# Batched matmul, 32 x (512 x 1024) x (1024 x 768): most output stores cover four batches instead of two

## The chip, the cores and the metric

The kernel runs on one core of a Trainium2 chip. A core has a matrix engine (PE), a vector engine (DVE), a scalar engine (ACT), a general engine (POOL) and a queue engine (SP), and 16 DMA engines that move data between the chip's memory (HBM) and the on-chip buffers (SBUF). Every engine runs its own list of instructions and waits on semaphores for the others. The metric is device time in microseconds (us). The kernel before takes 513.2 us, the median of three runs (512.89 to 513.69).

## The reference

```python
def setup_inputs():
    batch, m, k, n = 32, 512, 1024, 768
    return {
        "x": np.random.randn(batch, m, k).astype(np.float32),
        "weight": np.random.randn(batch, k, n).astype(np.float32),
    }

def reference(x, weight):
    return np.matmul(x, weight).astype(np.float32)
```

All three arrays are float32 in HBM. The kernel reads 167.77 MB and writes 50.33 MB.

## The kernel before, in words

**Work of one batch.** A batch has four tiles of 128 rows (MT = 4). PE needs x with k on the partitions, so it transposes x: the loads of x cast to bf16, two bf16 values are taken as one f32 word, and one transpose moves such words (line 169). DVE spreads the result into bf16 buffers `xT` (lines 229 to 255). Then PE multiplies (line 150): for each of the four tiles, eight slices of k, each in two matmuls of up to 512 columns, into PSUM buffers `pm`. ACT and DVE copy `pm` into an `out` buffer (lines 275 to 297).

**Batches go in pairs.** x is loaded for pairs of batches (1 and 2, 3 and 4, ..., 29 and 30, with 0 and 31 by themselves); on PE one round is the eight groups of transposes of such a pair, then batch 2k+1, then batch 2k+2 (`pair_on_pe`, line 175). Weights of batches 4 to 27 are loaded for pairs that begin with an even batch (4 and 5, ..., 26 and 27; line 100, a transfer whose shape is 128 x 2 x 6144), the others one by one (line 104). So a pair of weights is first needed by the second batch of a round. There are four weight buffers, two x buffers of a pair each, and four out buffers of a pair each (batches 2a and 2a+1 share out buffer a % 4; the rows are laid so that a partition holds 24,576 bytes that are contiguous in HBM).

**The stores.** `store` (line 123) waits until ACT and DVE have copied both batches of pair a and sends the pair in one transfer of 128 rows of 24,576 bytes, 3 MB. `slot_free` (line 257) makes ACT and DVE wait, before they refill an out buffer, until the store of its old contents has landed (semaphores `s_st`, one for each out buffer).

**The order of the transfers** is written out by hand in `on_pool` (line 324): nearly all DMA transfers are issued by POOL, in one queue, in program order. For every odd b it issues, one after the other, the load of x for round (b+3)/2, which waits until PE's transposes have emptied the x buffer (line 112); the store of pair a = (b-5)/2, for a from 0 to 10; and the weights of batches b+3 and b+4, which wait until PE has multiplied the batches whose buffers they take (lines 98 and 103). The stores of pairs 11, 12 and 13 are held back (HELD = 4) until all loads have been issued, at b = 28 (line 349). SP issues the first load of x, and at the end the store of pair 14 and four half stores of batches 30 and 31 (`on_sp`, line 353). At the end POOL waits for its stores and clears the semaphores (`clear_on_pool`, line 365).

Of the kernel before, what the change touches and what calls it, by code (L numbers as in the profile page):

```python
# [7 lines left out]
F32 = mybir.dt.float32  # L8
# [4 lines left out]
def kernel(  # L13
# [7 lines left out]
    B, M, K = x.shape  # L21
    _, _, N = weight.shape
    P = 128
    H = P // 2
    MT = M // P
# [3 lines left out]
    ROW = MT * N  # L29
    AHEAD = 3  # L30
    LATE = 4
    HELD = 4
    GROUPS = 2 * MT
    W_SLOTS, X_SLOTS, OUT_SLOTS = 4, 2, 4
# [3 lines left out]
    pe, dve, act, pool, sp = nc.tensor, nc.vector, nc.scalar, nc.gpsimd, nc.sync  # L38
# [3 lines left out]
    x_view = x.rearrange("b (mi mo) k -> b mi mo k", mi=P)  # L42
    pair_view = x[1:B - 1].rearrange("(p r) (mi mo) k -> p (r mi) mo k", r=2, mo=2 * MT)
    out_view = out.rearrange("b (mi mo) n -> b mi (mo n)", mi=P)
    two_view = out.rearrange("(p r) (i m) n -> p (r i) (m n)", r=2, m=2 * MT)

    def sbuf(name, shape, dtype):
        return nc.alloc_sbuf_tensor(name, shape, dtype).ap()
# [3 lines left out]
    ws = [all_ws[:, i] for i in range(W_SLOTS)]  # L52
    xs = [sbuf(f"x{i}", [P, 2 * MT, K], BF16) for i in range(X_SLOTS)]
    both = [sbuf(f"xT{i}", [P, 2, JT, 2, H, 2], BF16) for i in range(MT)]
    outs = [sbuf(f"out{i}", [P, 2 * ROW], F32) for i in range(OUT_SLOTS)]
    one = sbuf("one", [P, ROW], F32)
    x_first = outs[3][:, :MT * K].rearrange("p (mo k) -> p mo k", mo=MT)
    pts = [nc.alloc_psum_tensor(f"pt{i}", [P, JT, P], F32).ap() for i in range(2)]
# [6 lines left out]
    def sem(name):  # L65
        sems.append(nc.alloc_semaphore(name))
        return sems[-1]
# [7 lines left out]
    s_st = [sem(f"s_st{i}") for i in range(OUT_SLOTS)]  # L75
    s_fin = sem("s_fin")
# [9 lines left out]
    def out_done(b):  # L86
        return 2 * (b + 1)
# [4 lines left out]
    def together(b):  # L92
        return W_SLOTS <= b < B - W_SLOTS

    def load_w(b):
        if together(b):
            if b % 2 == 0:
                pool.wait_ge(s_mm, mm_done(b + 1 - W_SLOTS))
                slots = all_ws[:, b % W_SLOTS:b % W_SLOTS + 2].rearrange("p r ko n -> p r (ko n)")
                pool.dma_start(out=slots, in_=w_two_view[b // 2]).then_inc(s_w[b % W_SLOTS], 16)  # L100
            return
        if b >= W_SLOTS:
            pool.wait_ge(s_mm, mm_done(b - W_SLOTS))
        pool.dma_start(out=ws[b % W_SLOTS], in_=w_view[b]).then_inc(s_w[b % W_SLOTS], 16)  # L104

    def loads_of_w(b):

        return sum(not (together(i) and i % 2) for i in range(b % W_SLOTS, b + 1, W_SLOTS))

    def load_x(k):  # L110
        if k >= X_SLOTS:
            pool.wait_ge(s_pt, pt_done(k - X_SLOTS))
        slot = xs[k % X_SLOTS]
        if 2 * k + 1 == B - 1:
            pool.dma_start(out=slot[:, :MT], in_=x_view[B - 1]).then_inc(s_x[k % X_SLOTS], 16)
        else:
            pool.dma_start(out=slot, in_=pair_view[k]).then_inc(s_x[k % X_SLOTS], 16)  # L117

    def copied(eng, j):
        eng.wait_ge(s_ap, j + 1)  # L120
        eng.wait_ge(s_dp, j + 1)

    def store(eng, a, sem):
        copied(eng, out_done(2 * a + 1) - 1)
        eng.dma_start(out=two_view[a], in_=outs[a % OUT_SLOTS]).then_inc(sem, 16)  # L125

    def store_half(b, p):
        src = one if b == B - 2 else outs[(b // 2) % OUT_SLOTS]
        half = slice(p * N2, (p + 1) * N2)
        copied(sp, 2 * b + p)  # L130
        sp.dma_start(out=out_view[b, :, half], in_=src[:, half]).then_inc(s_fin, 16)
# [124 lines left out]

    def slot_free(eng, b):
        a = b // 2
        if a >= OUT_SLOTS and b % 2 == 0 and b < B - 2:
            eng.wait_ge(s_st[a % OUT_SLOTS], 16 * (a // OUT_SLOTS))  # L260
        if b == B - 1:
            eng.wait_ge(s_st[a % OUT_SLOTS], 16 * (a // OUT_SLOTS))

    def pieces(b, p, i):

# [9 lines left out]
    def out_on_act(b, p):  # L275
        j = 2 * b + p
        if p == 0:
            slot_free(act, b)
        act.wait_ge(s_mm, 2 * j + 1)
        for piece in pieces(b, p, 0):  # L280
            last = act.copy(*piece)  # L281
        last.then_inc(s_a, 1)
        act.wait_ge(s_mm, 2 * j + 2)
        act.copy(*pieces(b, p, 2)[0]).then_inc(s_ap, 1)  # L284

    def out_on_dve(b, p):
        j = 2 * b + p
        if p == 0:
            slot_free(dve, b)
        dve.wait_ge(s_mm, 2 * j + 2)  # L290
        if b >= B - 2:
            dve.tensor_copy(*pieces(b, p, 1)[0]).then_inc(s_dp, 1)  # L292
            return
        for piece in pieces(b, p, 1):
            last = dve.tensor_copy(*piece)  # L295
        last.then_inc(s_d, 1)
        dve.tensor_copy(*pieces(b, p, 2)[1]).then_inc(s_dp, 1)  # L297
# [22 lines left out]
    def landed(eng, slot, n, ready, uses=1):  # L320

        eng.wait_ge(slot, 16 * n).then_inc(ready, uses)

    def on_pool():
        load_w(0)
        pool.memset(ident, 0.0).then_inc(s_zero, 1)
        pool.wait_ge(s_zero, 1)
        pool.affine_select(
            out=ident,
            in_=ident,  # L330
            compare_op=mybir.AluOpType.not_equal,
            fill=1.0,
            base=0,
            pattern=[[-1, P]],
            channel_multiplier=1,
        ).then_inc(s_ident, 1)
        load_x(0)
        load_w(1)
        load_w(2)
        load_x(1)  # L340
        for b in range(B):
            if b % 2 and b + AHEAD + 1 < B:
                load_x((b + AHEAD) // 2)
            a = (b - 5) // 2
            if b % 2 and 0 <= a < B // 2 - 1 - HELD:
                store(pool, a, s_st[a % OUT_SLOTS])
            if b + AHEAD < B:
                load_w(b + AHEAD)
            if b == B - LATE:
                for a in range(B // 2 - 1 - HELD, B // 2 - 2):  # L350
                    store(pool, a, s_st[a % OUT_SLOTS])

    def on_sp():
        for b in range(B):
            if not (together(b) and b % 2):
                landed(sp, s_w[b % W_SLOTS], loads_of_w(b), s_wr, 1 + together(b))
        store_half(B - 2, 0)
        store(sp, B // 2 - 2, s_fin)
        store_half(B - 2, 1)
        store_half(B - 1, 0)  # L360
        store_half(B - 1, 1)
        sp.sem_inc(s_zero, 1)
        sp.wait_ge(s_fin, 80).then_inc(s_fin, -80)

    def clear_on_pool():

        for i, s in enumerate(s_st):
            pool.wait_ge(s, 16 * len(range(i, B // 2 - 2, OUT_SLOTS)))
        pool.wait_ge(s_zero, 2)
        used = range(sems[0].num, s_fin.num)  # L370
        pool.dma_reset(used)
        pool.sem_clear(used)

    with tc.tile_critical():
        sp.dma_start(x_first, x_view[0]).then_inc(s_first, 16)
        on_pool()
        on_pe()
        on_dve()
        on_act()
        on_sp()  # L380
        clear_on_pool()
# [30 lines left out]
```

## Time and profile before

| what | value |
|---|---|
| median of the runs | 513.2 us (512.89 to 513.69) |
| profiled execution, whole | 513.58 us |
| profiled execution, span | 511.8 us, 6037 instructions |
| PE matmul busy | 434.8 us (85%) |
| DVE, ACT, POOL busy | 207.0, 110.2, 29.8 us |
| DMA packets | 9611, 135.40 MB as written |
| HBM traffic | 167.77 MB read, 50.33 MB written: 426 GB/s over the span |
| mean granted PE clock | 0.946 |

The span is the time from the first to the last instruction in the profile; the whole execution is 1.8 us longer. Issues by line, with the size of one and the median time from issue to landing:

```profile
out_dram<-out POOLq DMA_DIRECT2D x14, 3072.0 KB, 29.7
w<-in_weight_dram POOLq DMA_DIRECT2D x12, 3072.0 KB, 34.1
x<-in_x_dram POOLq DMA_DIRECT2D x15, 2048.0 KB, 23.0
w<-in_weight_dram POOLq DMA_DIRECT2D x8, 1536.0 KB, 32.2
```

Sizes are those written to the target: a load of w or x reads twice as much, since it casts f32 to bf16. Times in views of the trace count from the span's start. A line such as "L150 MATMUL pm<-w,xT ... x63 [3.52 <-PEq L173]" is a group of 63 matmuls of line 150, before which PE was idle for 3.52 us until its own queue, waiting at line 173 for a load, let it go on.

### The profile page before, as it was taken

How to read it: one execution, taken by the hardware profiler on the slowest of the kernel's cores; microseconds unless marked ns; L12 is line 12 of the kernel's file. 1: busy time of each engine (PE TensorE's matmuls, PEld its weight loads, DVE VectorE, ACT ScalarE, POOL GpSimd, SP SyncE). 2: the span in 40 equal slices, each digit the busy share in tenths (PEclk: the TensorE clock that was granted, in tenths of full speed). 3: DMA queues.
4: the chain of work that ended last, by engine and by line, in shares of the span. 5: the costliest groups of instructions: out<-in, count | busy, mean ns of one | idle time of the engine just before them, and what ended most of it. 6: DMA issues, size and time to landing. Idle time of an engine off the chain costs nothing. (4 is left out here: it accounts for less than half of the span.)

```text
span 511.8 us, 6037 instructions
## 1 busy us (share of the span) xinstructions
PE 434.8 (85%) x2528; PEld 278.5 (54%) x2576; DVE 207.0 (40%) x332; ACT 110.2 (22%) x189; POOL 29.8 (6%) x56
## 2 busy tenths in 40 slices
PE   0899975999998698987979989699897988999993
PEld 0666642666565364653646546365463644666561
DVE  0463540545445063451533525235252451545330
ACT  1013120132222112221212221122211222132210
POOL 3000000000101000010000100001000010010000
PEclk9999995999999799997989989799898997999998
DMA  8999999999999999999999999999999999999997
GB/s 255 212 216 218 224 208 224 208 230 327 220 331 220 242 312 223 332 221 254 297 224 335 219 267 283 217 340 215 277 273 220 335 219 298 256 217 249 428 428 309
DMA packets 9611, 135.40 MB, mean 265 GB/s; under 512 B 896, under 2 KB 896, under 8 KB 1408
## 3 DMA queue, kind: packets, MB, share of 16 engines
q0 software_dynamic: 8736, 126.88, 96.4%
q1 hardware_dynamic: 864, 8.39, 4.0%
q8 instruction: 5, 0.08, 0.1%
q14 instruction: 6, 0.05, 0.0%
HBM read 167.77 MB, written 50.33 MB: 426 GB/s over the span
## 5 line engine op out<-in xcount | busy, mean ns | idle before, releaser
L150 PE MATMUL pm<-w,xT 128*128 128x256 bf16 (+1 forms) x2000 | 351.0, 336 | 44.9 <-PEq L173 42.4
L150 PEld LDWEIGHTS pm<-w,xT 128*128 128x128 bf16 x2048 | 205.7, 101 | 188.1 <-issue 63.2
L295 DVE COPY out<-pm 64x512 f32<-64x512 f32 x120 | 82.5, 687 | 200.7 <-PE pm L150 199.9
L281 ACT COPY out<-pm 64x512 f32<-64x512 f32 (+1 forms) x122 | 70.7, 580 | 294.7 <-PE pm L150 294.0
L249 DVE COPY xT<-pt 128x1024 bf16<-128x1024 bf16 x112 | 72.2, 687 | 61.0 <-PE pt L169 61.0
L169 PE MATMUL pt<-ident,x 128*128 128x128 f32 x496 | 79.9, 302 | 10.5 <-DVE xT L249 9.5
L169 PEld LDWEIGHTS pt<-ident,x 128*128 128x128 f32 x496 | 69.2, 209 | 21.8 <-DVE xT L249 17.5
L284 ACT COPY out<-pm 64x512 f32<-64x512 f32 (+1 forms) x62 | 35.8, 578 | 89.7 <-PE pm L150 89.7
L297 DVE COPY out<-pm 64x512 f32<-64x512 f32 x60 | 41.2, 686 | 0.0
L117 POOL DMA_DIRECT2D x<-in_x_dram x15 | 8.3, 555 | 271.1 <-PE pt L169 270.9
L169 PE MATMUL pt<-ident,out 128*128 128x128 f32 x32 | 6.7, 360 | 12.7 <-DMA out<-in_x_dram 12.3
L100 POOL DMA_DIRECT2D w<-in_weight_dram x12 | 8.4, 703 | 112.8 <-PE pm L150 112.8
L169 PEld LDWEIGHTS pt<-ident,out 128*128 128x128 f32 x32 | 5.1, 206 | 14.1 <-issue 12.3
L232 DVE CAST xT<-pt 128x256 bf16<-128x256 f32 x16 | 6.2, 440 | 14.0 <-PE pt L169 13.8
L125 POOL DMA_DIRECT2D out_dram<-out x14 | 7.5, 537 | 0.7 <-DVE out L297 0.7
L104 POOL DMA_DIRECT2D w<-in_weight_dram x8 | 4.4, 556 | 19.2 <-PE pm L150 18.1
L247 DVE COPY xT<-pt 128x512 bf16<-128x512 bf16 x8 | 3.4, 420 | 4.1 <-PE pt L169 4.1
L292 DVE COPY out<-pm 128x512 f32<-128x512 f32 x2 | 1.4, 692 | 8.4 <-PE pm L150 8.4
L252 DVE COPY xT<-pt 128x1024 bf16<-128x1024 bf16 x4 | 2.6, 686 | 5.2 <-PE pt L169 5.2
L248 DVE COPY xT<-pt 128x512 bf16<-128x512 bf16 x8 | 3.3, 415 | 0.0
L292 DVE COPY one<-pm 128x512 f32<-128x512 f32 x2 | 1.4, 686 | 3.2 <-PE pm L150 3.2
L281 ACT COPY one<-pm 128x512 f32<-128x512 f32 x2 | 1.2, 585 | 4.0 <-PE pm L150 4.0
(9 smaller groups left out, 3.9 us busy)
## 6 DMA issues: line engine op xcount, KB each, us to landing
out_dram<-out POOLq DMA_DIRECT2D x14, 3072.0 KB, 29.7
w<-in_weight_dram POOLq DMA_DIRECT2D x12, 3072.0 KB, 34.1
x<-in_x_dram POOLq DMA_DIRECT2D x15, 2048.0 KB, 23.0
w<-in_weight_dram POOLq DMA_DIRECT2D x8, 1536.0 KB, 32.2
out_dram<-out SPq DMA_DIRECT2D x1, 3072.0 KB, 18.5
out<-in_x_dram SPq DMA_DIRECT2D x1, 2048.0 KB, 11.3
out_dram<-one SPq DMA_DIRECT2D x2, 768.0 KB, 12.4
out_dram<-out SPq DMA_DIRECT2D x2, 768.0 KB, 8.2
```

Source lines behind the costliest of these rows:

```text
L100: pool.dma_start(out=slots, in_=w_two_view[b // 2]).then_inc(s_w[b % W_SLOTS], 16)
L104: pool.dma_start(out=ws[b % W_SLOTS], in_=w_view[b]).then_inc(s_w[b % W_SLOTS], 16)
L117: pool.dma_start(out=slot, in_=pair_view[k]).then_inc(s_x[k % X_SLOTS], 16)
L125: eng.dma_start(out=two_view[a], in_=outs[a % OUT_SLOTS]).then_inc(sem, 16)
L150: last = pe.matmul(pm[bank][:, at:at + size], xT[:, ko // 2, :, ko % 2], w[:, ko, off:off + size], start=(ko == 0), stop=(ko == KT - 1),)
L169: last = pe.transpose(pts[g % 2][:, i, :], rows, ident)
L232: last = dve.tensor_copy(xT[:, 2 * (g % 2) + j].rearrange("p (h i) r -> p r h i", h=2), pt[:, 2 * j:2 * j + 2].rearrange("p r (i h) -> p r ...
L249: return dve.tensor_copy(tile[:, :, :, half].rearrange("p b j i r -> p j b i r"), pt)
L281: last = act.copy(*piece)
L284: act.copy(*pieces(b, p, 2)[0]).then_inc(s_ap, 1)
L295: last = dve.tensor_copy(*piece)
L297: dve.tensor_copy(*pieces(b, p, 2)[1]).then_inc(s_dp, 1)
```

## The change

The four out buffers become one tensor, so that two neighbouring ones can be one operand. The stores follow a list: pairs (0, 1), (2, 3), (4, 5), (6, 7) and (8, 9) go in one transfer each, pairs 10 and 11 alone, pairs 12 and 13 together. A double store of pairs a and a+1 stands in POOL's order where the single store of pair a stood, so behind every second load of x; it waits for the copies of pair a+1 and counts on the semaphore of the first of its buffers. `await_store`, which `slot_free` calls, works out from the list which semaphore and count stand for a pair. Pairs 11 to 13 stay held back to b = 28, as two transfers. SP's stores are the same.

```diff
+    four_view = out.rearrange("(q s r) (i m) n -> q (r i) s (m n)", s=2, r=2, m=2 * MT)
...
-    outs = [sbuf(f"out{i}", [P, 2 * ROW], F32) for i in range(OUT_SLOTS)]
+    all_outs = sbuf("out", [P, OUT_SLOTS, 2 * ROW], F32)
+    outs = [all_outs[:, i] for i in range(OUT_SLOTS)]
...
-    def store(eng, a, sem):
-        copied(eng, out_done(2 * a + 1) - 1)
-        eng.dma_start(out=two_view[a], in_=outs[a % OUT_SLOTS]).then_inc(sem, 16)
+
+    STORES = [(a, 2) for a in range(0, B // 2 - 1 - HELD - 1, 2)]
+    STORES += [(B // 2 - 2 - HELD, 1), (B // 2 - 1 - HELD, 1), (B // 2 - HELD, 2)]
+
+    def store(eng, a, n, sem):
+        copied(eng, out_done(2 * (a + n - 1) + 1) - 1)
+        at = a % OUT_SLOTS
+        to, of = (four_view[a // 2], all_outs[:, at:at + 2]) if n == 2 else (two_view[a], outs[at])
+        eng.dma_start(out=to, in_=of).then_inc(sem, 16)
+
+    def store_on_pool(i):
+        a, n = STORES[i]
+        store(pool, a, n, s_st[a % OUT_SLOTS])
+
+    def await_store(eng, a):
+        first = next(i for i, n in STORES if i <= a < i + n)
+        done = sum(i % OUT_SLOTS == first % OUT_SLOTS for i, _ in STORES if i <= first)
+        eng.wait_ge(s_st[first % OUT_SLOTS], 16 * done)
...
-        if a >= OUT_SLOTS and b % 2 == 0 and b < B - 2:
-            eng.wait_ge(s_st[a % OUT_SLOTS], 16 * (a // OUT_SLOTS))
-        if b == B - 1:
-            eng.wait_ge(s_st[a % OUT_SLOTS], 16 * (a // OUT_SLOTS))
+        if b == B - 1 or (a >= OUT_SLOTS and b % 2 == 0 and b < B - 2):
+            await_store(eng, a - OUT_SLOTS)
...
             a = (b - 5) // 2
-            if b % 2 and 0 <= a < B // 2 - 1 - HELD:
-                store(pool, a, s_st[a % OUT_SLOTS])
+            for i, (first, _) in enumerate(STORES[:-2]):
+                if b % 2 and a == first:
+                    store_on_pool(i)
             if b + AHEAD < B:
                 load_w(b + AHEAD)
             if b == B - LATE:
-                for a in range(B // 2 - 1 - HELD, B // 2 - 2):
-                    store(pool, a, s_st[a % OUT_SLOTS])
+                store_on_pool(-2)
+                store_on_pool(-1)
```

In `clear_on_pool` POOL waits for as many completions of each semaphore as the list gives.

More of the change, by code (lines that the diff above doesn't have):

```diff
@@ L357, in on_sp @@
         store_half(B - 2, 0)
-        store(sp, B // 2 - 2, s_fin)
+        store(sp, B // 2 - 2, 1, s_fin)
         store_half(B - 2, 1)
@@ L367, in clear_on_pool @@
         for i, s in enumerate(s_st):
-            pool.wait_ge(s, 16 * len(range(i, B // 2 - 2, OUT_SLOTS)))
+            done = sum(a % OUT_SLOTS == i for a, _ in STORES)
+            if done:
+                pool.wait_ge(s, 16 * done)
         pool.wait_ge(s_zero, 2)
```

## The prediction

> **What bounds the kernel now.** I read the row of slices first, to see which resource is never free.
>
> ```profile
> PE   0899975999998698987979989699897988999993
> ...
> DMA  8999999999999999999999999999999999999997
> ...
> q0 software_dynamic: 8736, 126.88, 96.4%
> q1 hardware_dynamic: 864, 8.39, 4.0%
> ```
>
> PE has gaps in every part of the span; the DMA engines have none. The two data queues add up to 100.4% of 16 engines' span (packets overlap by some 20 ns, so a sum slightly over 100% is possible). Next the busy time by stretches: the loads, the stores that were held back, the end. Columns are busy us of PE, PEld, DVE, ACT and POOL, then clock, DMA share and GB/s.
>
> ```profile
> 5.00:474.00 469.00, 406.39 (x2356) 260.81 (x2401) 197.74 (x318) 101.92 (x176) 26.50 (x46) 0.95 1.02 255
> 474.00:508.00 34.00, 28.41 (x174) 17.74 (x176) 9.22 (x14) 7.00 (x12) 0.00 (x0) 0.99 0.99 424
> 508.00:511.80 3.80, 0.00 (x0) 0.00 (x0) 0.00 (x0) 0.00 (x0) 0.00 (x0) 0.50 0.17 73
> ```
>
> From the first packet (5.9 us) to 508 the engines' share is 0.99 to 1.02. So the time is the bytes, the order does not matter to first order, and the chain of waits (PE from 423.3 to 503) only runs beside it. That chain is still close, so PE's timeline comes third. Columns: start, duration, in brackets the idle time before.
>
> ```profile
> 392.00 11.95 PE L150 MATMUL pm<-w,xT 128*128 128x512 bf16 x63 [3.52 <-PEq L173]
> ...
> 409.66 10.35 PE L150 MATMUL pm<-w,xT 128*128 128x256 bf16 x62
> 423.48 13.24 PE L150 MATMUL pm<-w,xT 128*128 128x512 bf16 x63 [3.48 <-PEq L173]
> ...
> 442.45 20.75 PE L150 MATMUL pm<-w,xT 128*128 128x256 bf16 x125
> ```
>
> PE waits 3.52 and 3.48 us for weights before batches 24 and 26, runs the next batch at a lower clock (11.95 and 13.24 us against 10.56 undisturbed), and waits for no load after 423.48.
>
> The trace also marks each transfer's completion 16 times, once per DMA engine. Last marks (us), and in brackets the step from the transfer before:
>
> ```
> w8 137.92 (14.50)  x5 148.34 (10.42)  s1 155.61 (7.26)  w10 170.07 (14.47)
> w20 328.19 (14.51) w22 359.85         w24 391.67 (14.46) x13 401.42 (9.75)
> s9 408.70 (7.27)   w26 423.16 (14.46) w28 447.43 (7.25)  w31 474.14 (7.33)
> s11 481.43 (7.29)  s12 488.71 (7.28)  last half of out 507.68 (first) to 510.65 (last)
> ```
>
> (s is a store; w8 is the pair of batches 8 and 9.) One period is x 9.7 + store 7.3 + w 14.5 = 31.5 us; PE needs 26.6 of it.
>
> **The change, part by part.**
>
> *Bytes, and what stands before what.* Before w26 in POOL's queue stood stores 0 to 9; now stand (0,1) to (8,9), the same bytes. Store 10 and the three held ones keep their places. So w26 lands at 423.16 as before, and the sum of bytes gives 0.
>
> *Six stores fewer (14 to 8 on POOL).* The trace has no store of 256 packets. Nearest rows: w pairs have that shape (128 x 2 x 6144) and step 14.47; two single w step 2 x 7.25 = 14.50. Upper bound 14.53 to 14.46 against 14.50: a merge is worth -0.06 to +0.03 us, six are worth -0.35 to +0.2. I take **-0.15**. Long runs of stores cost nothing extra: s11 and s12, back to back at the end, step 7.29 and 7.28. POOL saves 14 x 0.54 - (6 x 0.70 + 2 x 0.54) = 2.3 us of issuing, which is off the path, since POOL waits for PE 9 to 27 us at a time.
>
> The Trainium skill ("DMA: Bandwidth & Descriptors", "Anatomy of one DMA") fits a transfer as 2.0 us plus its bytes; by that six transfers fewer would save an estimated 12 us. The rows above deny it here, where the queue is never empty: the merge of two w was worth 0.03.
>
> *Fewer turns from loading to storing.* An x ahead of no store steps 9.69 (x0, x1). The eleven ahead of a store (x4 to x14) step 9.70, 10.42, 9.73, 9.91, 9.74, 9.75, 10.02, 9.64, 10.11, 9.75, 9.69 on the slowest engine: 1.87 us over 11 x 9.69. Single packets at the ends of these x take 1.3 to 2.0 us instead of 1.23. Five of the eleven turns go. If the turn is the cause, 5/11 x 1.87 = 0.85 is saved; if it is something else (an instruction fetch of 0.31 us falls into x5), nothing. I take the middle, **-0.4**; bounds -1.0 and 0.
>
> *Waits of POOL, ACT and DVE.* A double store waits for the copies of batch 2a+3, behind an x that waits for transposes which PE makes after batch 2a+4: no new wait. Behind it on POOL stands a w that waits some 9 us for PE anyway. At the end the wait of 0.68 us for batch 27's copies now holds 6 MB instead of 3 MB, with 20 us of loads queued. Buffers: s0 lands at 123.42 + 7.28 = 130.7, and its buffer is refilled by batch 8, whose weights stand behind the store in the queue, so the store is always the earlier. Ring space: 63 descriptors an engine are outstanding at 455 us now, some 50 at most in the loop afterwards.
>
> *PE's waits.* Every second w (w8, w12, ... w24) lands 7.28 later; the others land as before. So PE waits about 7.5 us every second pair and not at all in the other, in place of 3.5 us each. The last long wait is batch 24: w24 lands at 391.67 + 7.28 = 398.95, batch 24 starts 0.3 later at 399.2. Waits over 5 us cost the next batch 2.0 to 2.9 us in clock (13.13, 13.49, 12.59 against 10.56); I take 2.5. Transposes and batch 25 take 16.05 (392.00 + 11.95 to 420.0). Batch 26 starts at 399.2 + 13.06 + 16.05 + 0.2 = 428.5, with w26 there since 423.2, hence at full clock, and ends 10.4 later at 438.9, where it ended at 436.6. PE is **2.3 us late** for the rest, 1.8 if w24 gains the 0.5 above. What hides that: SP issues the last half of out at 498.59 + 5.46 - 0.33 = 503.7; the first engine has landed it at 507.68, but the slowest, busy without a gap, at 510.65. So 2.97 us of lateness fit before the slowest engine has nothing to do. Cost 0; if the cover were gone, 2.3.
>
> The Trainium skill ("TensorE: Matmul & The Clock Gate", "Why this matters for your kernels") speaks against the change: no PE gaps over some 3 us, or the clock halves. The rows hold that price already, and it lies in the 2.5; by the page's window of 3.4 us at half rate I would estimate 1.7 and a lateness of 1.5, the same result.
>
> *Sum*: 0 - 0.15 - 0.4 + 0 = -0.55. The profiled execution took 513.58 (span 511.8, 1.8 around it), which gives 513.0; it stands 0.4 over the median of 513.2, so **the forecast is 512.7**, no change that a measurement of this kernel can tell (about 0.2%, 1.0 us).
>
> **Rivals.**
>
> *The turns cost more than I allow (faster).* All eleven excesses gone with the merges, 0.85 to 1.0, plus 0.35 for six merges: -1.2 to -1.4, 512.0 to 511.8. For: the long packets stand only at the ends of x that precede stores. Against: instruction fetches explain some; and PE's lateness caps it, as the end cannot come before 507.68 + 1.3 plus the engines' spread.
>
> *The queue runs dry behind a storeless x (slower).* Without a store DMA needs 24.2 us a pair, PE 29 after a long wait, and x is only issued when PE's transposes are through. For pair 11: w20 lands at 328.19 + 7.28 = 335.47, batch 20 starts at 335.8, and x12 is issued 18.9 later (347.43 - 328.51 now), at 354.7. The queue ends with w22, on the fastest engine at 357.08, on the slowest at 359.85: 2.4 and 5.1 us of cover. From issue to first packet SP's first load took 1.0 us (0.95 to 1.96), POOL's first, cold, 4.4 (1.47 to 5.88); no warm one shows, as the queue is never empty. I take it near the lower end, 1.5 to 2: dry nowhere, or briefly on the fast engines, which are not the bound. The rival decides from 5.1: at 4.4 plus a clock loss of 3.4 in place of 2.4 it is 0.3 short, and some 1 us with an engine further ahead, five times: +1.5 to +5, 514.2 to 517.7 after the gains.
>
> *PE becomes the end (slower, small).* A clock loss of 3.4 makes it 3.2 late against 2.97: +0.2. Only a second slow batch, 2.5 more, gives +2.5: 515.2. Against: from 428 on PE waits for nothing.
>
> *The merged transfer is cut into smaller packets (slower).* Four packets of 6144 bytes take 4 x 0.234 = 0.936 us, one of 24576 takes 0.912: +0.19 a store, 12 stores +2.3, 515.0. Against: merged pairs of w have the same packets (12288 bytes written) as single w.
>
> **How the numbers follow.** Forecast (within 0.2% of 513.2) 0.50; turns and merges at full price 0.27; dry queue, late PE or smaller packets 0.23. The range takes in the bounds (-1.4 below) and the cheaper half of the dry queue (+1.5 to +2): 511.8 to 515.0. For the forecast alone, 512.2 to 514.2.
>
> **What would show it.** Right: w26 still lands near 423, DMA stays at 9 in every slice, PE's waits go to about 7.5 us at five places and vanish between them, double stores step near 14.55, the chain starts at batch 24 near 399 and ends some 2 us later, x ahead of w steps 9.7. Wrong: a digit under 9 in the DMA row in mid-span (dry queue), a store step over 14.6, a last half issued after 506.7 with the end moved likewise, or w26 landing over 1 us early (turns dearer than thought).

## The result, and the profile after

The changed kernel takes 514.15 us (median of 22 runs: 21 of 513.28 to 516.84, and a slow one of 521.42 that the comparison and the spread leave out) against 513.37 us (22 runs of the kernel before, 512.89 to 513.93). The ratio is 1.0021, with a 95% interval of 1.0013 to 1.0029: slower by 0.2%. More telling than the median is the spread: 3.6 us where the kernel before has 1.0.

The profiled execution took 516.84 us, span 515.1, so it is one of the slow ends of that spread, 3.3 us over the profile of before. The page of the changed kernel, the same rows as before:

```profile
PE   0899975999669995799957999489994899999993
...
DMA  8999999999999999999999999999999999999997
...
q0 software_dynamic: 8640, 126.88, 96.4%
q1 hardware_dynamic: 864, 8.39, 4.0%
```

The DMA engines are as busy as before, in every slice, with 96 packets fewer (six transfers fewer, each with one packet of 4 bytes on each of 16 engines). Yet the same bytes take 3.3 us longer. The stretches of the changed kernel (busy us of PE, PEld, DVE, ACT, POOL, then clock, DMA share, GB/s):

```profile
5.00:474.00 469.00, 398.34 (x2377) 256.90 (x2378) 196.14 (x316) 100.75 (x174) 24.31 (x40) 0.94 1.02 253
474.00:508.00 34.00, 32.30 (x201) 20.01 (x199) 10.72 (x17) 8.16 (x14) 0.00 (x0) 1.00 1.00 422
508.00:511.80 3.80, 0.00 (x0) 0.00 (x0) 0.00 (x0) 0.00 (x0) 0.00 (x0) 1.00 0.85 356
```

Up to 474 us the share is 1.02 as before, and the rate 253 GB/s instead of 255. So busy engines moved fewer bytes. Where? The completion marks say it. Landing step of the x loads on the slowest engine (us over 9.69), and the cover: the time from the issue of x to the first landing of the transfer ahead of it, that is, how long the queue still has work when x is issued.

```
changed kernel, this profile        x4    x6    x8    x10   x12   x14     x5 x7 x9 x11 x13
cover                               4.67  3.77  2.54  3.26  2.33  1.36    15.3 to 17.0
loss, slowest engine                0.06  0.58  1.30  0.04  1.52  1.71    -0.00 to 0.01
loss, mean of the 16 engines        0.05  0.07  1.03  0.02  0.98  1.82    -0.01 to 0.01
```

The slowest engine loses 5.2 us in the six x that a store follows; in the kernel before it lost 1.9 in eleven, with covers of 3.6 to 13.4. The difference is 3.3 us, the whole of the longer span. The last load (w31) lands at 477.45 instead of 474.14, the last store at 513.93 instead of 510.65.

How such a load looks. Two stretches of the changed kernel, at the start and in the middle of x14, one at its end:

```profile
421.00:424.00 3.00, 3.00 (x20) 1.83 (x19) 1.25 (x2) 1.16 (x2) 0.55 (x2) 1.00 1.01 184
424.00:429.00 5.00, 5.00 (x33) 3.05 (x32) 1.99 (x3) 1.74 (x3) 0.00 (x0) 1.00 1.00 213
429.00:433.00 4.00, 4.00 (x27) 2.42 (x25) 1.99 (x3) 0.86 (x2) 0.53 (x1) 1.00 1.09 186
```

The last number is the one to read: 184 and 186 GB/s as written at both ends, 213 between, with a share of 1.00 or more throughout. The same 5 us in the middle of x14 in the kernel before:

```profile
423.50:428.50 5.00, 5.00 (x16) 2.29 (x17) 0.00 (x0) 0.00 (x0) 0.00 (x0) 0.50 1.00 213
```

The packets are in work, but some take 1.5 to 3.0 us instead of 1.23. They come in two bursts: 10 long packets at the start of x (from 421.2 on, 0.42 us for each of the 16 engines on average) and 26 at its end, ahead of the store (from 429.2 on, 1.27 us an engine).

And why the cover is short, on PE and POOL of the changed kernel:

```profile
400.88 13.07 PE L167 MATMUL pm<-w,xT 128*128 128x512 bf16 x64 [9.06 <-PEq L190]
...
419.45 20.96 PE L167 MATMUL pm<-w,xT 128*128 128x512 bf16 x128
```

```profile
392.11 0.70 POOL L102 DMA_DIRECT2D w<-in_weight_dram  x1 [9.85 <-PE pm L167]
419.91 0.57 POOL L119 DMA_DIRECT2D x<-in_x_dram  x1 [27.10 <-PE pt L186]
420.48 0.55 POOL L133 DMA_DIRECT2D out_dram<-out  x1
```

In the kernel before POOL's rows for the same two loads were:

```profile
388.77 0.70 POOL L100 DMA_DIRECT2D w<-in_weight_dram  x1 [9.31 <-PE pm L150]
409.91 0.56 POOL L117 DMA_DIRECT2D x<-in_x_dram  x1 [20.43 <-PE pt L169]
```

PE waits 9.06 us for w24 behind the double store, runs batch 24 with a lowered clock (13.07 us, at a granted clock of 0.80), then transposes, and only then can POOL issue x14, at 419.91, when w26 is nearly through: it lands from 421.27 on. In the kernel before x14 was issued at 409.91, 10.5 us before w26 began to land.

### The profile page after: what moved, and what is told of

Its sections match the earlier page's. It is cut to its first block, busy times and chain, and to the rows that moved or that the text cites. A ratio compares the mean times of both kernels' runs of the same rounds, so it can differ in the third digit from the quotient of the medians.

```text
span 515.1 us, 6073 instructions
## 1 busy us (share of the span) xinstructions
PE 430.6 (84%) x2576; PEld 276.9 (54%) x2576; DVE 206.9 (40%) x332; ACT 110.2 (21%) x189; POOL 27.6 (5%) x50
## 5 line engine op out<-in xcount | busy, mean ns | idle before, releaser
L186 PE MATMUL pt<-ident,x 128*128 128x128 f32 x496 | 80.0, 302 | 10.5 <-DVE xT L266 9.5
L133 POOL DMA_DIRECT2D out_dram<-out x8 | 5.3, 666 | 1.3 <-DVE out L312 1.3
```

The source lines that it names most:

```text
L133: eng.dma_start(out=to, in_=of).then_inc(sem, 16)
L186: last = pe.transpose(pts[g % 2][:, i, :], rows, ident)
```

## The experiments

Four theories. **D**: x comes late to a short queue, and then loses time. **T**: turning from a load to a store costs, whatever the lateness. **S**: the shape of the merged store does. **I**: POOL's issuing of the next weights disturbs the DMA engines; the bursts at the ends of x8, x12 and x14 fell on such issues.

### The changed kernel again

> The changed kernel once more, for a second profile. What its first profile suggests: nearly all of the added time is in x loads that a store follows (x6 +0.6, x8 +1.3, x12 +1.5, x14 +1.7 us of landing step over 9.69; x5, x7, x9, x11, x13 none), in bursts in which all engines' packets grow. If these bursts are a matter of chance, this profile has them in another number, and its span follows that number: 511.5 us with none, about 1 us more for each. If they are fixed, the same four loads are long again and the span is near 515.

Measured: 514.51 us (12 runs, 513.29 to 518.45), ratio 1.0032 (1.0012 to 1.0052). Profile: span 514.5, long loads x10 (1.54 on the slowest engine, cover 2.17) and x14 (1.36, cover 2.34), while x8 (cover 3.12) and x12 (3.26) lose 0.1 or nothing. So which loads are long is a matter of chance, but not of blind chance: it goes with the cover. The expected 511.5 plus about 1 us for each burst fits roughly. All x ahead of a store lose 4.0 us on the slowest engine (x4 and x6 some 0.5 each), 2.1 more than in the kernel before, and the last load lands 2.1 later (476.27); the span is 2.7 longer, and where the other 0.6 arose is not shown.

### Two single stores at the place of each double one

```diff
-            if b % 2 and 0 <= a < B // 2 - 1 - HELD:
-                store(pool, a, s_st[a % OUT_SLOTS])
+            if b % 2 and a % 2 == 0 and 0 <= a < B // 2 - 1 - HELD:
+                for i in range(a, min(a + 2, B // 2 - 1 - HELD)):
+                    store(pool, i, s_st[i % OUT_SLOTS])
```

> Each double store of the changed order is issued as two single stores of 128 packets, one behind the other, at the same place of POOL's queue. Theory S (the shape: 256 packets of two buffers are slow or disturb): as the kernel before, ratio 1.000, no long x loads. Theory O (the order: x is issued late in rounds without a store, and w is issued while x runs): as the change, ratio 1.001 to 1.003, with the long x loads.

Measured: 514.51 us (513.39 to 518.42), ratio 1.0030 (1.0015 to 1.0046), with x10, x12 and x14 long (1.42, 1.89, 1.97; covers 2.61, 1.41, 1.58). Theory S falls: without a single merged transfer the loss is the same. It is the order.

### Weights issued later, and the store ahead of x

The first is the changed kernel with two more tiles in the wait for w:

```diff
-                pool.wait_ge(s_mm, mm_done(b + 1 - W_SLOTS))
+                late = 2 if b % 4 == 0 and 8 <= b else 0
+                pool.wait_ge(s_mm, mm_done(b + 1 - W_SLOTS) + late)
...
-            pool.wait_ge(s_mm, mm_done(b - W_SLOTS))
+            pool.wait_ge(s_mm, mm_done(b - W_SLOTS) + (2 if b == 29 else 0))
```

> The changed kernel, but in rounds with a store POOL issues the weights half a batch (5.2 us) later, when the queue is already in the store. Theory I (POOL writing the descriptors of w while the queue is in the last part of x stalls the engines; the burst at 239 us fell on the issue at 238.9, those at 365 and 430 likewise): the bursts at the ends of x go, ratio 0.999 to 1.000. Theory D (x comes late to the queue): the x starts stay as they are, ratio 1.001 to 1.003. Theory T (the turn from loading to storing itself): as the change.

Measured: 514.46 us (513.25 to 517.21), ratio 1.0021 (1.0009 to 1.0032), bursts at the ends of x12 (1.23 us an engine) and x14 (1.03) although no w is issued there now: w24 goes out at 370.84 and w29 at 435.78, when these bursts are over. (In the round of x14 only w29 is held back; w28 still follows the store at once.) Theory I falls for the bursts at the ends.

In the second the loop of `store_on_pool` stands ahead of `load_x`:

```diff
+            a = (b - 5) // 2
+            for i, (first, _) in enumerate(STORES[:-2]):
+                if b % 2 and a == first:
+                    store_on_pool(i)
             if b % 2 and b + AHEAD + 1 < B:
                 load_x((b + AHEAD) // 2)
-            a = (b - 5) // 2
-            for i, (first, _) in enumerate(STORES[:-2]):
-                if b % 2 and a == first:
-                    store_on_pool(i)
```

> The changed kernel with the double store ahead of x in POOL's queue instead of behind it, so that the queue holds 14.6 us more when the late x is issued, and w is issued while the store runs. Theory D (x late): no long x, ratio 0.998 to 1.000. Theory I: the same. Theory T (the turn from x to a store): bursts go from x, but may appear ahead of the store in w, 1.000 to 1.003. Theory S (the shape): as the change, 1.002.

Measured: 513.50 us, and a spread of 0.35 us (11 runs, 513.37 to 513.72); ratio 1.0001 (0.9992 to 1.0010). POOL's rows of this kernel:

```profile
391.88 0.70 POOL L102 DMA_DIRECT2D w<-in_weight_dram  x1 [9.84 <-PE pm L167]
392.57 0.58 POOL L133 DMA_DIRECT2D out_dram<-out  x1
417.23 0.54 POOL L119 DMA_DIRECT2D x<-in_x_dram  x1 [24.08 <-PE pt L186]
```

The store now goes out with the weights, 25 us ahead of x14, and bridges the time in which PE is late: covers are 10.2 to 19.6 and no x loses anything. The bursts that T allowed ahead of the store show mainly in two w: w10 and w26 step 15.77 and 14.97 us on the slowest engine instead of 14.53. Theory D expects this; T allowed it too, since no x is followed by a store any more. The next four separate these two.

### x issued later, in the order of before

```diff
             pool.wait_ge(s_pt, pt_done(k - X_SLOTS))
+            if 4 <= k < B // 2 - 1:
+                pool.wait_ge(s_mm, mm_done(2 * k - 4) + 2)
```

with 2, 3 and 4 tiles. Nothing else differs from the kernel before.

> The kernel before, with its single stores and its order, but each x that a store follows (x4 to x14) is issued two tiles (5.2 us) later. Cover is the time from the issue of x to the first landing of the transfer ahead of it, the time at which the fastest engine has nothing else to do; it is 9.7 to 12.6 us in the kernel before, so 4.5 to 7 here. Theory D (x loses when its cover is under some 3 us, as 18 loads of the changed order show): as before, ratio 1.000. Theory T (the turn or the merged order is what costs): as before, 1.000.

Measured: 518.67 us, ratio 1.0103 (1.0085 to 1.0121). I had overlooked x4, whose cover is only 3.63 in the kernel before: it fell to -1.28, the queue ran empty, and x4 alone lost 4.25 us on the mean of the engines. The other ten, with covers of 3.9 to 8.4, lost 0.00 to 0.08. So the expected time was missed and the expected rule held.

> The same with three tiles (7.8 us), which leaves 1.9 to 4.8 us of cover. Theory D: about half of the eleven loads fall under 3 us and lose some 1 us each, 516 to 520 us, with the same bursts of long x packets at the start and the end of those loads. Theory T: nothing of the order has changed, 513.4.

Measured: 525.31 us, ratio 1.0235 (1.0218 to 1.0251). x4 lost 6.73 (cover -3.80); x10, x12 and x14 lost 1.40, 2.01 and 2.19 (covers 2.31, 0.91, 1.30); the other seven, above 3.4, at most 0.21.

> The same with four tiles (10.4 us), cover -0.7 to 2.2 us, so that the queue is empty ahead of x. Theory D: all eleven loads lose 1 to 3 us, 524 to 540 us, less what PE's waits give back. Theory T: 513.4.

Measured: 539.26 us, ratio 1.0523 (1.0484 to 1.0561). x4 9.69; eight more, with covers of 0.8 to 2.6, lost 1.7 to 2.5 each, in two bursts; x5 and x7 (covers 8.4 and 3.5) nothing. Theory T has no room for any of the three.

All x loads ahead of a store, from the nine profiles with such loads (74 loads):

```
cover, us       loads   loss of a mean engine, us (least to most)
under 0            3    4.25 to 9.69
0.8 to 1.7        13    1.54 to 2.53   mean 2.00
1.7 to 2.9         9    0.22 to 1.83   mean 1.13
2.9 to 3.5         7   -0.01 to 0.29   mean 0.13
3.5 to 5          17    0.00 to 0.10
over 5            25   -0.01 to 0.42
```

The 0.42 is x12 of the kernel before, with a cover of 9.65: a small burst at its end, which the cover does not explain. Of the two bursts the first needs the shorter cover. Counting packets over 0.15 us too long, the 13 loads with covers of 0.8 to 1.7 have 0.29 to 1.04 us an engine at the start and 0.71 to 1.66 behind it; the eight with covers of 2.0 to 2.7 have 0.00 to 0.25 at the start and 0.44 to 1.47 behind it. So at the covers of x8 and x12 in the changed kernel nearly the whole loss lies at the end, ahead of the store.

### PE kept at work through its long waits

Only PE's list changes: while it waits for w behind a double store, it runs 42 matmuls from `xT` buffers into a free transpose buffer. Nobody reads them. `warm` is set in the second round of each turn of PE's loop, except for its last turn, which now stands behind the loop.

```diff
-    def pair_on_pe(k, q):
+    def pair_on_pe(k, q, warm=False):
...
         for r in range(2):
+            if r and warm:
+                for i in range(42):
+                    pe.matmul(
+                        pts[0].rearrange("p j m -> p (j m)"),
+                        both[0][:, 0].rearrange("p j h i r -> p j (h i) r")[:, 0, :, 0],
+                        both[1][:, 0].rearrange("p j h i r -> p (j h i r)")[:, :512],
+                        start=True,
+                        stop=True,
+                    )
             take(s_wr)
...
```

> The changed kernel with its order of transfers untouched; while PE waits for the weights in the second round of each turn of its loop it runs 42 matmuls whose results nobody reads (9.1 us), so that its clock does not fall and the next x is issued some 2.5 us earlier. The last two rounds stand behind the loop without them. Theory D: cover rises from 1.4 to 4.7 to about 4 to 7 us, the long x loads go, ratio 1.000 with a spread as narrow as before's. Theory T: the loads stay long, 1.002 with the wide spread.

Measured: 513.36 us (513.15 to 513.73), ratio 0.9997 (0.9988 to 1.0006). PE and POOL of this kernel around x14:

```profile
387.99 9.23 PE L203 MATMUL pt<-xT 128*128 128x512 bf16 x42
398.14 10.56 PE L167 MATMUL pm<-w,xT 128*128 128x512 bf16 x64 [0.92 <-PEq L190]
```

```profile
414.66 0.57 POOL L119 DMA_DIRECT2D x<-in_x_dram  x1 [25.51 <-PE pt L186]
```

Batch 24 takes 10.56 us instead of 13.07, x14 is issued at 414.66, its cover is 5.27 instead of 1.36, and it loses 0.04. All six x ahead of a store have covers of 5.3 to 5.8. With the order of the transfers, the merged stores and the turns untouched, the loss and the spread are gone. Nor is it the lowered clock itself: in the kernel before PE's granted clock was 0.50 from 423.5 to 428.5 us, in the midst of x14, and that x14, with its cover of 10.5, lost nothing. This run, with the three of x issued later, settles theory D: without the lateness there is no loss. It also points to where the chance came from, the length of the batch behind each long wait. In the second profile of the changed kernel the batches of 11.96, 12.59 and 12.02 us leave the x behind them (x6, x8, x12) covers of 4.37, 3.12 and 3.27, those of 13.48 and 12.95 leave x10 and x14 2.17 and 2.34; the first profile has 11.96 to 13.36.

### Whose is the burst at the end of x?

The store behind the weights: first as a control, then with x issued late.

```diff
             a = (b - 5) // 2
-            if b % 2 and 0 <= a < B // 2 - 1 - HELD:
-                store(pool, a, s_st[a % OUT_SLOTS])
             if b + AHEAD < B:
                 load_w(b + AHEAD)
+            if b % 2 and 0 <= a < B // 2 - 1 - HELD:
+                store(pool, a, s_st[a % OUT_SLOTS])
```

> Single stores as before, but behind the weights instead of behind x: the order is x, w, store. x keeps a cover of some 14 us or more and no store follows it. Theory D: nothing is lost, ratio 1.000, narrow spread. Theory T says the same here; the run is the control for the next.

Measured: 516.45 us, ratio 1.0059 (1.0035 to 1.0082): missed. No x loses anything (covers 4.2 to 19.7), but the ends of w, now ahead of a store, have small bursts, and they tell most on the engine that lands last: w12, w16, w20 and w22 step 15.15, 15.50, 15.17 and 15.06 there against 14.53, and the eleven w ahead of a store lose 4.4 us together (the eleven x of the kernel before 1.9). The lag of the last engine behind the first grows to 5.3 us (2.8 in the kernel before), and the last landing comes at 513.0. So some of theory T is true: turns into a store cost a little even with a full queue, and in this profile more behind w than behind x.

The late version adds a wait to x:

```diff
             pool.wait_ge(s_pt, pt_done(k - X_SLOTS))
+            if 5 <= k < B // 2 - 1:
+                pool.wait_ge(s_mm, mm_done(2 * k - 3) + 2)
```

> The same order, with x5 to x14 issued only when PE has done half of the next batch, so that their cover is about -1 to 2 us, and with w, not a store, behind them. It asks what the burst of long packets at the end of a late x belongs to. If it belongs to the lateness, each x loses 1.5 to 2.5 us in two bursts as in the run with x four tiles late, and the time is 530 us or more. If it belongs to the turn to a store that was issued just behind, only the burst at the start stays (0.5 to 0.8 us an engine) and the losses are about half.

Measured: 566.47 us, ratio 1.1032 (1.1012 to 1.1052). The covers came out at -0.8 to -6.5, less than meant, so most of the loss is an empty queue: x5 to x14 lose 3.0 to 8.5 each. What was asked can still be read. Around x8 in this kernel, POOL's issue and two stretches:

```profile
251.28 0.53 POOL L119 DMA_DIRECT2D x<-in_x_dram  x1 [33.66 <-PE pm L152]
...
250.00:252.00 2.00, 1.95 (x13) 1.19 (x13) 0.90 (x2) 0.90 (x2) 0.72 (x2) 1.00 0.00 0
252.50:256.00 3.50, 3.50 (x25) 2.30 (x24) 0.58 (x1) 1.55 (x4) 0.57 (x2) 1.00 1.22 215
```

Share 0.00: the queue is empty; x8 was issued at 251.28 and its first packets start at 252.5. Each x has a burst of 0.5 to 0.7 us an engine at its start and none at its end. The second burst (0.9 to 1.2 us an engine) has moved to the end of w, ahead of the store. So the first burst belongs to the late load, the second to the turn to a store behind it, and the second is this large only when the loads ahead of it began with a short queue (at most about 1 us on the slowest engine in the control). What the changed kernel pays is thus in the main a turn to a store behind a late load. One rival of the first burst is not tested: POOL issues the next transfer 0.5 to 1.3 us behind x, about when the first packets of a late x start (1.2 to 1.5 us behind). What in the DMA engines makes either burst, no run here shows.

## Why the prediction was wrong, point by point

*What bounds.* Right: the DMA engines are the bound, and the order of bytes ahead of w26 did not matter by itself.

*Merged stores (-0.15) and fewer turns (-0.4).* The kernel with PE kept at work has both and no late x; it stands at -0.03% (-0.12 to +0.06%), between -0.6 and +0.3 us. The -0.55 lies at the edge of that, so it is neither shown nor refuted. For the merge the steps speak: double stores step 14.52 to 14.57 us, two single ones 14.5 to 14.7, so nothing measurable was gained. For the turns one profile of each kernel speaks: the six x ahead of a store lose 0.8 us on the slowest engine with PE kept at work, the eleven of the kernel before 1.9; the last load lands 0.9 us earlier, the last store 0.35. Some readings behind these terms were off without deciding anything: x2 and x3, which no store follows either, step 9.74 and 9.84, so not every excess is a turn's; the lower bound of a merge by its own rows (14.46 against 14.50) is -0.04 and not -0.06; and by the packets of the trace some 41 per engine, not 63, were outstanding at 455 us.

*PE's waits.* The mechanism was right in every link: long waits at every second w, none between, a lowered clock behind each, x issued late (x12 at 355.25, worked out as 354.7). The covers of x12 were put at 2.4 and 5.1 us on the fastest and the slowest engine; they are 2.33 and 5.03. The waits are 8.3 to 9.1 us rather than 7.5.

*The step that failed* stands in the rival of the dry queue: "dry nowhere, or briefly on the fast engines, which are not the bound. The rival decides from 5.1". I priced a late x only by the time in which an engine would have nothing to do. Measured, a load of POOL needs some 1.2 us from issue to first packet, less than the 1.5 to 2 that I took and less than the shortest cover of the changed kernel's profile (1.36), so the queue did not run dry; but an x issued less than about 3 us ahead of the first landing loses up to 2.5 us (on average 2.0 at covers of 0.8 to 1.7 and 1.1 at 1.7 to 2.9), on the slowest engine as on the others, while they count as busy. With covers that I had worked out as 2.4, two or three loads in a profiled execution are hit, 1 to 2 us each. That turned a forecast of -0.55 into +0.8 in the median and +3.3 in the profiled execution. That the median still lies within 511.8 to 515.0 is luck: the upper part of the range stood for a queue that runs dry, and in these profiles it did not run dry.

*PE's lateness at the end.* Put at 2.3 with 2.97 to spare. In the profile the last half was issued at 507.4 (503.7 before), 3.7 late; but the last load and the last landing both moved by 3.3, what the x loads had lost. The cover at the end held, so this term was rightly put at nothing.

*What would show it.* "DMA stays at 9 in every slice" came true and was no sign of health. "A digit under 9" was the wrong watch for this rival; the rate at full share was the right one. The sign "a last half issued after 506.7 with the end moved likewise" did appear (507.4, the end 3.3 later), but it stood for PE's lateness, and the x loads had moved both.

## What to carry to other kernels

Merging or regrouping transfers in one queue also regroups the waits of the engine that releases the next ones: look for the transfer that is then issued last before the queue runs out, and count its lead. Here a lead under 3 us cost time although the queue never ran empty; putting a long transfer that waits for nothing ahead of the late one (the store ahead of x) mended it for free. And when a change leaves the best time alone but widens the spread, look for a race between two engines that a clock or a wait decides.

## What the runs showed of the hardware that was not expected

- DMA engines at a busy share of 1.01 to 1.09 moved 184 to 186 GB/s as written in a load that runs at 213 in its middle: packets that take longer count as busy all the while, so the share alone does not tell the rate.
- From POOL's issue to the first packet some 1.2 us with an empty queue (251.28 to 252.5, and 1.22 to 1.24 us for ten such loads), yet loads ahead of a store needed about 3 us of lead here to lose next to nothing.
- Turning from w to a store cost the engine that lands last up to 1.0 us at a time even with a full queue (4.4 us in eleven turns), and the time ends with the engine that lags most (5.3 us against 2.8).
- A store of 256 packets, 6 MB, steps 14.52 to 14.57 us, twice a single one (7.25 to 7.35).
